# A convolution tile whose pads change places: one POOL copy less, one written by ScalarE from PSUM instead

## The chip, the cores and the metric

The kernel runs on one core of one Trainium2 chip. The metric is the time of one execution on the device in microseconds (us). TensorE (PE in the profile) multiplies matrices and writes PSUM; VectorE (DVE), ScalarE (ACT) and GpSimd (POOL) work elementwise; SyncE (SP) issues the DMAs. Each engine takes its own instructions strictly in the order of the program and waits on semaphores for the others.

## What is computed

The reference is one inference step of a small hybrid decoder: a Mamba-2 layer, an attention layer, and an MLP behind each. There are 1024 prompt tokens, 8 samples of 8 new tokens, and 16 meta tokens that stand ahead of the prompt. Only the first layer's causal convolution is touched by the change:

```python
def mamba_mixer(h, conv_state, ssm_state, norm_w, w_in, conv_w, conv_b, ...):
    zxbcdt = rmsnorm(h, norm_w) @ w_in
    ...
    xpad = jnp.concatenate([conv_state.astype(xbc.dtype), xbc], axis=1)
    new_conv = xpad[:, L:]
    conv = conv_b
    for k in range(CONV_K):
        conv = conv + xpad[:, k:k + L] * conv_w[k]
    xbc = jax.nn.silu(conv)
    ...
```

`CONV_K` is 4, so each output needs the three inputs before it. For a sample these are three rows of `state_conv`. For the meta tokens they are zeros. For the prompt they are the last three meta rows, since the prompt goes on from the meta tokens' state. `new_conv`, the last three inputs, is an output for the prompt and for each sample.

## The kernel before

Features lie on the 128 partitions and tokens along the columns: columns 0 to 1023 are the prompt, then 64 sample columns, then 16 of meta, 1104 in all (`T`). PE works on three chunks of columns, `CH`: 384, 384 and 336, the last with 256 prompt columns and the 80 others. The fp32 products are made as three products of split halves (`mm3`, L205 to L207), 24 matmuls for a unit's chunk.

The work before some 680 us is `mixer` (L1956). It goes through 8 groups, and each has four *units* of 128 features: B, C, x0 and x1. A unit is made so:

- `conv_unit` (L553) takes its weights, a tile `xp` of two buffers for the unpadded product with its pads, and a tile `fm` (called `acc` there) for the result.
- `conv_mm` (L560) makes a chunk's product in one of three PSUM banks `g`. Chunks go in the order 2, 0, 1 (`CORD`), so the samples and meta tokens come first.
- `conv_out` (L583) empties the bank with ScalarE. L588 copies prompt columns to `xp`. For the chunk with the others L590 copies the 80 columns into ten blocks of eight, each behind three columns of pad. L592 writes the last tap and the bias into `acc`, and with that the bank is free.
- `conv_rest` (L595) has POOL fill the pads and the output `cvo` of new states: L600 puts the samples' states into blocks 0 to 7, L601 puts zeros ahead of the first meta block (8), L602 copies the end of block 8 ahead of the second meta block (9), L603 copies the end of block 9 ahead of the prompt, and L604 and L605 copy the new states out. Then DVE does three short taps over the 80 columns (L608), three long taps over the 1024 (L611), and the gate (L615) around ScalarE's tanh (L614).

The state-space part of a group, `ssd` (L627), runs beside the units of the *next* group. It is a recurrence over nine stretches of tokens (first the 80 others, then eight of 128), made of small PE matmuls: transposes into `tp` (L647 to L649), `cb` (L659), `y` (L675 and L679), the carried state through `st` (L701, L708; DVE adds it at L703 and L713, POOL scales it at L710). For the samples, PE makes their state update in `st` (L767, L768), POOL scales the old state `h` in four pieces (L759), and DVE adds the two (L769). There is one PSUM bank `st`, so L767 and L708 wait until the last user of `st` is read. POOL also makes `xd` (L657) and `bm` (L754) and ends the output `yt` (L694). In the last group the gate's units take the place of the convolution's (`gate_group`, L773): their products meet DVE at L788, L789 and L797, and a sum over features goes through ScalarE (L248), DVE (L249) and PE (L260, L263).

What sets the order: the kernel is written as a stream of operations, and a scheduler places them on each engine by a simulated time line, each as early as its inputs and buffers allow there. The order of an engine is then fixed, and semaphores do the rest. So a change of one operation can move others on every engine.

## Time and profile before

| | before |
|---|---|
| time, median of 3 runs | 2843.23 us (2842.11 to 2844.07) |
| the profiled execution | 2845.32 us, span of its instructions 2843.6 us |
| mean granted TensorE clock | 0.995 |
| busy: PE, DVE, ACT, POOL | 98%, 73%, 49%, 17% of the span |
| instructions on POOL | 659 |

In the profile, busy is the union of an engine's instructions. PE's ends are modelled, so that neighbouring matmuls overlap: the distance from start to start is what one costs. "Idle before" is the time that the engine stood still ahead of an instruction, and the name behind the arrow is what ended that wait. An instruction between two long ones can show a wait that costs nothing, because only waits that reach PE move the end here. Instructions with fp32 operands count twice on PE. All times within the execution are from the span's start.

### The profile page before, as it was taken

How to read it: one execution, taken by the hardware profiler on the slowest of the kernel's cores; microseconds unless marked ns; L12 is line 12 of the kernel's file. 1: busy time of each engine (PE TensorE's matmuls, PEld its weight loads, DVE VectorE, ACT ScalarE, POOL GpSimd, SP SyncE). 2: the span in 40 equal slices, each digit the busy share in tenths (PEclk: the TensorE clock that was granted, in tenths of full speed). 3: DMA queues.
4: the chain of work that ended last, by engine and by line, in shares of the span. 5: the costliest groups of instructions: out<-in, count | busy, mean ns of one | idle time of the engine just before them, and what ended most of it. 6: DMA issues, size and time to landing. Idle time of an engine off the chain costs nothing.

```text
span 2843.6 us, 51263 instructions
## 1 busy us (share of the span) xinstructions
PE 2788.5 (98%) x19861; PEld 2690.4 (95%) x19861; DVE 2069.6 (73%) x3603; ACT 1392.0 (49%) x2721; POOL 476.2 (17%) x659
## 2 busy tenths in 40 slices
PE   8999999999999999999999999999999999999998
PEld 7999989988999999999999999988989999999998
DVE  6788878887768786666578875676678666577785
ACT  6555555555664355445343334555545445433333
POOL 3355555552000100000000022110110000000011
PEclk9999999999999999999999999999999999999999
DMA  4354444456755223533654533447553444543332
GB/s 140 93 149 125 129 121 111 126 147 206 272 204 183 91 93 128 182 129 129 238 212 173 178 115 91 165 167 255 169 181 115 157 159 149 201 153 132 128 124 78
DMA packets 219467, 433.41 MB, mean 152 GB/s; under 512 B 30728, under 2 KB 128392, under 8 KB 216648
## 3 DMA queue, kind: packets, MB, share of 16 engines
q1 hardware_dynamic: 219224, 430.14, 45.4%
q8 instruction: 156, 2.56, 0.4%
q14 instruction: 87, 0.71, 0.1%
HBM read 302.71 MB, written 128.32 MB: 152 GB/s over the span
## 4 chain that ended last, share of the span: by engine, by line
PE 82%; DVE 7%; DMA 5%; issue 2%; ACT 2%; POOL 1%; SPq 0%; POOLq 0%; DVEq 0%; ACTq 0%
PE g L206 11%; PE g L205 11%; PE g L207 11%; PE ma L205 4%; PE mc L205 4%; PE mc L207 4%; PE mc L206 4%; PE ma L207 4%; PE ma L206 4%; PE mb L207 3%; PE mb L206 3%; PE md L206 3%; PE mb L205 3%; PE md L207 3%; PE md L205 3%
## 5 line engine op out<-in xcount | busy, mean ns | idle before, releaser
L205 PE MATMUL g<-S,w 128*128 128x384 f32 (+2 forms) x1584 | 534.0, 337 | 3.6 <-DMA w<-ws_up 2.0
L206 PE MATMUL g<-S,w 128*128 128x384 f32 (+2 forms) x1584 | 532.3, 336 | 0.0
L207 PE MATMUL g<-S,w 128*128 128x384 f32 (+2 forms) x1584 | 531.1, 336 | 0.0
L205 PEld LDWEIGHTS g<-S,w 128*128 128x128 f32 x1584 | 300.0, 189 | 7.1 <-issue 3.9
L1091 ACT CAST w<-s 128x384 fp32r<-128x384 f32 (+1 forms) x272 | 150.4, 557 | 318.1 <-DVE s L1222 56.9
L206 PEld LDWEIGHTS g<-S,w 128*128 128x128 f32 x1584 | 300.5, 190 | 3.3 <-issue 2.6
L207 PEld LDWEIGHTS g<-S,w 128*128 128x128 f32 x1584 | 300.9, 190 | 2.5 <-issue 1.8
L1342 POOL TENSOR_TENSOR hh<-hh,us 128x552 f32<-128x552 f32 (+1 forms) x24 | 42.5, 1789 | 1528.8 <-DVE us L1318 872.8
L205 PE MATMUL ma<-S,w 128*128 128x276 f32 (+1 forms) x808 | 233.6, 289 | 4.0 <-DVE us L1318 2.7
L206 PE MATMUL ma<-S,w 128*128 128x276 f32 (+1 forms) x808 | 233.2, 289 | 0.3 <-DVE S L1280 0.3
L207 PE MATMUL ma<-S,w 128*128 128x276 f32 (+1 forms) x808 | 233.4, 289 | 0.0
L1092 DVE TENSOR_TENSOR w<-s,w 128x384 fp32r<-128x384 f32 (+1 forms) x272 | 166.5, 616 | 81.2 <-ACT w L1091 81.2
L1091 ACT CAST w<-raw 128x384 fp32r<-128x384 f32 (+1 forms) x204 | 112.2, 556 | 180.0 <-PE mc L207 54.1
L171 ACT CAST w<-raw 128x1024 fp32r<-128x1024 f32 x96 | 100.6, 1048 | 140.4 <-PE g L206 48.7
L172 DVE TENSOR_TENSOR w<-raw,w 128x1024 fp32r<-128x1024 f32 x96 | 123.0, 1281 | 48.4 <-ACT w L171 30.1
L206 PE MATMUL g<-R,w 128*128 128x384 f32 (+2 forms) x480 | 158.1, 329 | 0.0
L205 PE MATMUL g<-R,w 128*128 128x384 f32 (+2 forms) x480 | 158.0, 329 | 0.0
L207 PE MATMUL g<-R,w 128*128 128x384 f32 (+2 forms) x480 | 157.7, 329 | 0.0
L205 PEld LDWEIGHTS ma<-S,w 128*128 128x128 f32 x808 | 152.1, 188 | 4.9 <-ACT w L1091 3.1
L206 PEld LDWEIGHTS ma<-S,w 128*128 128x128 f32 x808 | 152.2, 188 | 0.5 <-DVE S L1280 0.5
L207 PEld LDWEIGHTS ma<-S,w 128*128 128x128 f32 x808 | 152.1, 188 | 0.0
L206 PE MATMUL mc<-S,w 128*128 128x276 f32 (+1 forms) x512 | 148.0, 289 | 0.7 <-DVE S L1280 0.7
(488 smaller groups left out, 8506.6 us busy)
## 6 DMA issues: line engine op xcount, KB each, us to landing
raw<-in_w_up_dram SPq DMA_DIRECT2D x64, 512.0 KB
raw<-in_w_in_dram SPq DMA_DIRECT2D x48, 512.0 KB
raw<-in_w_downs_dram SPq DMA_DIRECT2D x64, 384.0 KB
w<-ws_o SPq DMA_DIRECT2D x46, 512.0 KB
w<-ws_q SPq DMA_DIRECT2D x40, 512.0 KB
ab<-acs_d SPq DMA_DIRECT2D x64, 256.0 KB
S<-t_d SPq DMA_DIRECT2D x18, 828.0 KB
S<-t_e SPq DMA_DIRECT2D x18, 816.0 KB
```

Of the source, the lines that this page charges most:

```text
L171: nc.scalar.copy(out=wh, in_=raw)
L172: nc.vector.tensor_tensor(out=wl, in0=raw, in1=wh.bitcast(F32), op=ALU.subtract)
L205: mm(out=out, lhsT=wh, rhs=xh, start=(first and k == 0), stop=False)
L206: mm(out=out, lhsT=wh, rhs=xl, start=False, stop=False)
L207: mm(out=out, lhsT=wl, rhs=xh, start=False, stop=(k == n - 1))
L1091: self.last_hi = nc.scalar.copy(out=t[:, 0], in_=src).ins
L1092: self.last_lo = nc.vector.tensor_tensor(out=t[:, 1], in0=src, in1=t[:, 0].bitcast(F32), op=ALU.subtract).ins
L1342: e.tensor_tensor(out=to, in0=to, in1=uv, op=ALU.add)
```

## The change

The two parts of `xp` change places. Before, it held the pad and the prompt first (`XB` = 1027 columns) and then the ten padded blocks of samples and meta (110 columns). After it, the ten blocks come first (`XB` = 110) and the prompt's 1024 columns follow directly. Block 9 ends with the last eight meta rows, so the three columns ahead of the prompt are by themselves its pad, and the copy L603 goes. The pad of block 9, the last three rows of block 8, is written by ScalarE straight from the PSUM bank in `conv_out`, a copy of 128x3 behind the one of 128x80, and POOL's copy L602 goes. The taps read the same number of columns from their new places, and the tile has 1134 columns where it had 1137.

```diff
-XB = 3 + SEQ
-XW = XB + 110
+XB = 110
+XW = XB + SEQ
...
-        nc.scalar.copy(out=xp[:, 3 + o:3 + o + m], in_=pt[:, :m])
+        nc.scalar.copy(out=xp[:, XB + o:XB + o + m], in_=pt[:, :m])
         if m < n:
-            nc.scalar.copy(out=xp[:, XB:XW].rearrange("p (b e) -> p b e", e=11)[:, :, 3:11],
-                           in_=pt[:, m:n].rearrange("p (b q) -> p b q", q=8))
+            tail = xp[:, :XB].rearrange("p (b e) -> p b e", e=11)
+            nc.scalar.copy(out=tail[:, :, 3:11], in_=pt[:, m:n].rearrange("p (b q) -> p b q", q=8))
+            nc.scalar.copy(out=tail[:, 9, 0:3], in_=pt[:, m + 69:m + 72])
...
-        tail = xp[:, XB:XW].rearrange("p (b e) -> p b e", e=11)
+        tail = xp[:, :XB].rearrange("p (b e) -> p b e", e=11)
         nc.gpsimd.tensor_copy(out=tail[:, 0:8, 0:3], in_=cv[:, j, 5:29].rearrange("p (b k) -> p b k", k=3))
         nc.gpsimd.memset(tail[:, 8, 0:3], 0.0)
-        nc.gpsimd.tensor_copy(out=tail[:, 9, 0:3], in_=tail[:, 8, 8:11])
-        nc.gpsimd.tensor_copy(out=xp[:, 0:3], in_=tail[:, 9, 8:11])
-        nc.gpsimd.tensor_copy(out=self.cvo[:, j, 0:3], in_=xp[:, SEQ:SEQ + 3])
+        nc.gpsimd.tensor_copy(out=self.cvo[:, j, 0:3], in_=xp[:, XW - 3:XW])
...
-            nc.vector.scalar_tensor_tensor(out=acc[:, :SEQ], in0=xp[:, k:k + SEQ], scalar=cv[:, j, k:k + 1],
+            nc.vector.scalar_tensor_tensor(out=acc[:, :SEQ], in0=xp[:, XB - 3 + k:XB - 3 + k + SEQ], scalar=cv[:, j, k:k + 1],
```

Counted over the 32 units, POOL loses 64 copies, ScalarE gains 32, and every other instruction stays. The scheduler places the work anew on all engines from the first units (about 34 us of the profile before) to the end of the mixer (about 675 us); behind that the orders are equal. The lines below `conv_rest` move up by one, so L769 of before is L768 after. Three places matter below.

The first is the fifth group's sample states, at about 390 to 405 us of the profile before. On POOL stood, ahead of and behind the scaling of the old state (L759; its tile `h_4444` is one group's state):

```order
L754 TENSOR_TENSOR bm<-bhl,bsel 128x1024
L694 TENSOR_TENSOR yt<-yt,yo 128x256
L759 TENSOR_TENSOR h_4444<-h_4444,eendb 128x8x64 x4
L710 TENSOR_TENSOR hT<-hT,eend 128x256
L604 COPY cvo<-xp 128x3
L602 COPY xp<-xp 128x3
L603 COPY xp<-xp 128x3
L605 COPY cvo<-xp 128x24
```

There stands now, on the same engine at the same place:

```order
L693 TENSOR_TENSOR yt<-yt,yo 128x256
L656 TENSOR_TENSOR xd<-xdt,de 80x256
L753 TENSOR_TENSOR bm<-bhl,bsel 128x1024
L758 TENSOR_TENSOR h_4424<-h_4424,eendb 128x8x64 x4
L709 TENSOR_TENSOR hT<-hT,eend 128x256
L603 COPY cvo<-xp 128x3
L604 COPY cvo<-xp 128x24
```

The sum into `yt` has moved ahead of `xd` and `bm`, and of the copies only the two into `cvo`, which nothing on DVE waits for, are left. DVE at this place, before:

```order
L661 TENSOR_TENSOR cbm<-cb,tri 128x128
L611 SCALAR_TENSOR_TENSOR fm<-xp,cv,fm 128x1024
L738 TENSOR_TENSOR yo<-pp,ef 128x64 x2
L608 SCALAR_TENSOR_TENSOR fm<-xp,cv,fm 128x80 x2
L769 TENSOR_TENSOR h_4444<-h_4444,st 128x512
L608 SCALAR_TENSOR_TENSOR fm<-xp,cv,fm 128x80
L615 SCALAR_TENSOR_TENSOR fm<-th,fm 128x1104
```

And now:

```order
L660 TENSOR_TENSOR cbm<-cb,tri 128x128
L607 SCALAR_TENSOR_TENSOR fm<-xp,cv,fm 128x80
L737 TENSOR_TENSOR yo<-pp,ef 128x64 x2
L607 SCALAR_TENSOR_TENSOR fm<-xp,cv,fm 128x80 x2
L614 SCALAR_TENSOR_TENSOR fm<-th,fm 128x1104
L768 TENSOR_TENSOR h_4424<-h_4424,st 128x512
```

The short taps and the gate of the unit now stand ahead of the state update. On PE the product that waits for this update (L767) has 13 more of the large matmuls ahead of it than before.

The second place is PE at about 661 to 665 us, near the end of the last group. Before:

```order
L768 MATMUL st<-xdl,bm 128x256
L679 MATMUL y<-fm,hT 128x128 x2
L708 MATMUL st<-xd,Bt 128x256
L260 MATMUL g<-msh,ones_r 128x384
L205 MATMUL g<-S,w 128x336
L206 MATMUL g<-S,w 128x336
```

Now:

```order
L767 MATMUL st<-xdl,bm 128x256
L678 MATMUL y<-fm,hT 128x128 x2
L260 MATMUL g<-msh,ones_r 128x384
L205 MATMUL g<-S,w 128x336
L206 MATMUL g<-S,w 128x336
```

The product into `st` (L708, now L707) stands 22 large matmuls further on, and the sum over features (L260) comes first.

The third place is POOL at the start of the last group's recurrence, about 606 to 616 us. Before:

```order
L694 TENSOR_TENSOR yt<-yt,yo 128x256
L657 TENSOR_TENSOR xd<-xdt,de 80x256
L759 TENSOR_TENSOR h_7088<-h_7088,eendb 128x8x64 x4
L754 TENSOR_TENSOR bm<-bhl,bsel 128x1024
L710 TENSOR_TENSOR hT<-hT,eend 128x256
```

Now:

```order
L693 TENSOR_TENSOR yt<-yt,yo 128x256
L758 TENSOR_TENSOR h_7056<-h_7056,eendb 128x8x64 x4
L656 TENSOR_TENSOR xd<-xdt,de 80x256
L753 TENSOR_TENSOR bm<-bhl,bsel 128x1024
L656 TENSOR_TENSOR xd<-xdt,de 128x256
```

The scaling has moved ahead of the 80-row product `xd`, from which PE makes the first carried state (L701).

## Prediction

> **What bounds the kernel now.** First the page: span, engines, and the chain that ended last.

> ```profile
> span 2843.6 us, 51263 instructions
> PE 2788.5 (98%) x19861; PEld 2690.4 (95%) x19861; DVE 2069.6 (73%) x3603; ACT 1392.0 (49%) x2721; POOL 476.2 (17%) x659
> PE 82%; DVE 7%; DMA 5%; issue 2%; ACT 2%; POOL 1%; SPq 0%; POOLq 0%; DVEq 0%; ACTq 0%
> ```

> TensorE is the bound, and POOL, which loses work, carries 1% of the chain. Next the windows of the first 680 us, because the changed functions run only in the mixer: the copies of the first row below last from 34 to 591 us. In the other rows the columns are the window, its length, and busy us with instruction counts for PE, weight loads, DVE, ACT and POOL, then the granted clock and DMA.

> ```profile
> L588 ACT COPY xp<-g x96: 348/471/488, 34.2 to 591.2; 128x384 f32<-128x384 f32 x64, 128x256 f32<-128x256 f32 x32
> ...
> 100.00:200.00 100.00, 100.00 (x690) 92.10 (x690) 80.21 (x140) 57.61 (x139) 56.35 (x76) 1.00 0.50 133
> 400.00:500.00 100.00, 97.36 (x655) 90.19 (x654) 77.81 (x136) 52.84 (x124) 48.98 (x80) 0.98 0.45 130
> 600.00:680.00 80.00, 72.77 (x482) 65.38 (x481) 65.42 (x123) 41.90 (x95) 31.73 (x36) 0.98 0.49 143
> ```

> In most of the mixer PE has no idle time at all, so taking work from POOL, DVE or ACT is worth nothing there. What can be won is the 2.6 us in the window from 400 and part of the 7.2 us in the last 80. The waits of PE up to 680 us name them (engine, tile and line, releaser, us in total, times, longest):

> ```profile
> PE st L708 <- DVE h L769: 3.2, 1, 3.2
> PE st L767 <- DVE h L769: 3.0, 2, 2.6
> PE g L260 <- ACT msh L248: 2.5, 2, 1.7
> ```

> The second row holds the stall at 402 us. The timelines of PE, DVE and POOL at that place show its cause.

> ```profile
> 401.99 0.34 PE L206 MATMUL g<-S,w 128*128 128x384 f32 x1
> 404.98 0.39 PE L767 MATMUL st<-xdh,bm 128*128 128x256 f32 x1 [2.64 <-DVE h L769]
> ...
> 398.54 0.34 DVE L738 TENSOR_TENSOR yo<-pp,ef 128x64 f32<-128x64 f32 x2
> 403.39 0.93 DVE L608 SCALAR_TENSOR_TENSOR fm<-xp,cv,fm 128x80 f32<-128x80 f32 x2 [4.51 <-POOL xp L602]
> 404.25 0.68 DVE L769 TENSOR_TENSOR h<-h,st 128x512 f32<-128x512 f32 x1
> ...
> 391.81 5.73 POOL L694 TENSOR_TENSOR yt<-yt,yo 128x256 f32<-128x256 f32 x1 [1.40 <-DVE yt L690]
> 397.50 5.03 POOL L759 TENSOR_TENSOR h<-h,eendb 128x512 f32<-128x512 f32 x4
> 402.49 0.61 POOL L710 TENSOR_TENSOR hT<-hT,eend 128x256 f32<-128x256 f32 x1
> 403.05 0.18 POOL L604 COPY cvo<-xp 128x3 f32<-128x3 f32 x1
> 403.18 0.18 POOL L602 COPY xp<-xp 128x3 f32<-128x3 f32 x1
> ```

> A copy of 0.18 us stood in POOL's queue behind 11 us of other work. DVE waited 4.51 us for it at the tail's taps (L608). The state update L769, next in DVE's queue, came late, and PE, whose L767 needs the bank that L769 frees, stood still for 2.64 us.

> The stall has a second price. The clock column, window by window:

> ```profile
> 402.00:405.00 3.00, 0.36 (x3) 0.03 (x2) 1.57 (x4) 0.54 (x1) 2.23 (x9) 1.00 0.23 53
> 406.40:409.80 3.40, 3.40 (x16) 2.96 (x16) 0.88 (x2) 0.27 (x1) 0.61 (x1) 0.51 0.06 10
> 409.80:413.20 3.40, 3.40 (x28) 3.23 (x25) 2.41 (x6) 2.63 (x6) 1.20 (x2) 1.00 0.07 11
> 662.40:665.80 3.40, 1.23 (x7) 1.18 (x8) 3.40 (x9) 1.56 (x4) 0.45 (x1) 0.99 0.63 243
> 665.80:669.20 3.40, 3.40 (x14) 3.40 (x13) 3.40 (x7) 0.52 (x1) 1.93 (x3) 0.50 0.83 302
> ```

> From 406.4 us on the granted clock was 0.51 for 3.4 us, and the same followed the long stall near 662 us. About half the matmuls fit: an estimate of 3.4 x (1 - 0.51) = 1.7 us lost at most. I take 1.5.

> **The change, part by part.** *Removed from POOL*: 32 L602 and 32 L603. The groups by line (count | busy us, mean ns | idle before):

> ```profile
> L602 POOL COPY xp<-xp 128x3 f32<-128x3 f32 x32 | 13.0, 406 | 0.3 <-DVE xdt L652 0.3
> L603 POOL COPY xp<-xp 128x3 f32<-128x3 f32 x32 | 7.8, 242 | 0.0
> DVE fm L608 <- POOL xp L602: 10.3, 11, 4.5
> ```

> That is 20.8 us of POOL, worth nothing by itself, and 10.3 us of DVE's waiting in 11 places (last row). Ten of them never reached PE. The eleventh is the stall at 402 us. What is late there next? L769 also needs POOL's L759, which ended at 402.53 and does not go away. So L769 can end at about 402.53 + 0.68 = 403.2 rather than 404.93. In the new order 13 more matmuls stand ahead of this L767, at 0.18 us from start to start (two neighbours, below), or 2.3 us. PE gets there at about 404.4, after L769. The wait should vanish.

> ```profile
> 615.03 0.34 PE L206 MATMUL g<-S,w 128*128 128x384 f32 x1
> 615.21 0.34 PE L207 MATMUL g<-S,w 128*128 128x384 f32 x1
> 617.21 0.44 PE L260 MATMUL g<-msh,ones_r 128*128 128x384 f32 x1 [1.65 <-ACT msh L248]
> ...
> 608.73 4.05 POOL L759 TENSOR_TENSOR h<-h,eendb 128x512 f32<-128x512 f32 x4
> ```

>  The row's other 0.4 us (one L767 near 263 us) is covered in the same way by 5 matmuls. **-3.0 us**, between -3.0 and 0: nothing if L759 is held up longer, and no further gain exists in this row. With the stall its slow clock goes: **-1.5 us**, between -1.7 and 0, since other stalls may sit in another phase.

> [...] Here the clock fell after a stall of 2.64 us, so in this trace a mostly idle window sufficed. [...]

> *Added to ScalarE*: 32 copies of 128x3 from PSUM, between the 128x80 copy and the activation that closes the bank. The nearest rows:

> ```profile
> 34.50 0.23 ACT L590 COPY xp<-g 128x80 f32<-128x80 f32 x1
> 34.62 0.65 ACT L592 ACTIVATE fm<-g,cv 128x336 f32<-128x336 f32 x1
> ```

> The 128x80 copy lasted 0.23 us but held the next instruction back by only 0.12 us. For 32 copies that is 3.8 us (7.4 us by the duration). I take 0.12 as what ScalarE's queue sees. ScalarE is 53 to 58% busy here and PE has three banks to turn over, so the bank's release 0.12 us later is hidden: **0**. Without that cover it would be +3.8 us; it cannot fall below zero, since nothing leaves this queue. The tail's taps now wait for this copy instead of POOL's. It lies directly behind the copies they need anyway, so nothing long is queued ahead.

> *Moved*: the pad and the sequence change places in one tile. The sequence taps read as many columns as before, so they stay at their price: **0**. What POOL still writes ahead of the taps (the sample states and zeros) depends only on the buffer being free, as before.

> *Reordered*: the scheduler places everything anew up to 675 us, not beyond. Most of PE's dependent small matmuls come 3 to 15 large ones later, which is slack. In the order of the whole mixer I count 12 more switches between large and small matmuls; eight of these are y blocks that are followed directly by a large one. **+0.5 us**, an estimate, between 0 and 2. In the last 80 us the order around PE's longest wait changes:

> ```profile
> 663.20 0.50 ACT L248 CAST msh<-gt 128x384 fp32r<-128x384 f32 x1
> ...
> 663.85 0.67 DVE L769 TENSOR_TENSOR h<-h,st 128x512 f32<-128x512 f32 x1
> ...
> 664.57 0.70 PE L708 MATMUL st<-xd,Bt 128*128 128x256 f32 x2 [3.15 <-DVE h L769]
> ```

> L708 now stands behind L260 and 22 matmuls, so L769 has time. L260, which stands first now, needs L248, whose end at 663.70 leaves a wait of about 2.3 us where there were 3.15: **-1.0 us**. In return the last group starts its recurrence later: POOL's scaling of the carried state (4.05 us at 608.73, above) now stands ahead of the 80-row product that starts it. I count **+0.5 us** for a wait that opens near 629 us, between 0 and +4, the length of that POOL block. The tail's bounds are then -4.7 (both stalls and the second slow clock) and +4.

> Sum: -3.0 - 1.5 + 0.5 - 1.0 + 0.5 = **-4.5 us**. The profiled execution took 2845.3 us (span 2843.6 and 1.7 around it), 2.1 above the runs' median, so it would come to 2840.8, and the median of 2843.2 to **2838.7 us**.

> **The rivals.** *Given back (2843 us)*: the 402 us stall goes but the new order opens others of like size, since a wait of 2 us anywhere in 640 us suffices. For it: PE waits for several kinds of small result in every group, and each place was set anew. Against it: most of them moved later, and before, with the same work, the waits table has one wait of over 2 us that lies ahead of the last 80 us. -4.5 + 4.3, about 2843.

> *The tail gains too (2834 us)*: L708's stall goes with its slow clock, and L260's wait of 1.65 us at 617.21 shrinks because POOL's scaling starts earlier there. -4.5 - 2.3 - 1.5 - 0.9 = -9.2. For it: 22 matmuls are plenty. Against it: DVE is busy in all 3.40 us of the window from 662.4, and something must wait for it.

> *POOL starved (2849 us, slower)*: DVE no longer pauses at L608, and those pauses are when POOL's two-input work got through. The row of the added squares shows how the two engines hold each other up:

> ```profile
> L797 DVE TENSOR_TENSOR gt<-gt x6: 500/668/4796, 608.4 to 682.1; 128x384 f32<-128x384 f32 x4, 128x336 f32<-128x336 f32 x2
> ```

> One of six took 4.80 us beside POOL's scaling, as L694 took 5.73 us beside DVE. The scaling stands between the bank's update and PE in each of 8 groups. If it is starved once more in three groups by 3 to 4 us beyond the 1 to 2 us of slack, PE loses about 2.5 us in each and has a slow clock in two: 7.5 + 3.0 - 4.5 = +6.0, 2849.2. It decides from about 2 us of delay on. [...] Against the rival: 20.8 us of POOL's own work go.

> *The clock is not the stall's doing (2840 us)*: it fell 1.4 us after PE had started again (404.98 to 406.4) and may fall once more somewhere here whatever PE does. Then only the wait is saved: -4.5 + 1.5 = -3.0, 2840.2. [...] Against it: both slow windows of the table stand right behind PE's two longest waits.

> **How the numbers follow.** Forecast 0.45, given back 0.22, tail gains 0.17, starved 0.11, clock independent 0.05. What a measurement of this kernel can tell from no change is about 0.2%, 5.7 us: below 2837.5 is faster, above 2848.9 slower. Faster: the tail's case, and a third of the forecast's (its terms reach -7), 0.32. Slower: most of the starved case and a little of the given-back, 0.09. Same: 0.59. The range runs from the tail's case, 2834.0, to 2846.0, which takes in the given-back case with 3 us of spread and leaves out the starved one.

> **What would show it.** Right: no wait of 2 us at L767 in the fifth group, DVE not waiting for POOL at the tail's taps, no granted clock near 0.5 between 400 and 420 us, POOL some 20 us less busy, and the end of the mixer 3 to 5 us earlier. Wrong: a new wait of PE for the state update, long two-input POOL instructions, or the gain lost again behind the mixer, whose order is unchanged.

## The result and the profile after

The changed kernel took 2834.23 us in the median of five runs (2828.37 to 2835.08), the kernel before 2843.23 in five beside them (2840.14 to 2845.05). The ratio is 0.9962, with a 95% interval of 0.9951 to 0.9973: some 0.4% faster, 9.0 us by the medians and 10.8 by the ratio. The forecast was -4.5 us. First the page of the profiled execution, which was the shortest of its five runs (2828.37 us, 5.9 below their median), so the 17.3 us between the two spans say too much:

```profile
span 2826.3 us, 51212 instructions
...
PE 2780.6 (98%) x19861; PEld 2686.2 (95%) x19861; DVE 2068.0 (73%) x3603; ACT 1391.9 (49%) x2753; POOL 469.9 (17%) x595
...
PE 87%; DVE 5%; DMA 4%; ACT 2%; issue 1%; POOL 0%; SPq 0%; POOLq 0%; DVEq 0%; ACTq 0%
```

PE has gone from 82% to 87% of the chain, and POOL from 1% to none. POOL is 6.3 us less busy, not 20. The waits of PE up to 680 us (in the changed kernel the lines behind the convolution have numbers one lower: L768 is the L769 of before, L766 and L767 the old L767 and L768, L707 the old L708; ScalarE's new copy is L592):

```profile
PE g L260 <- ACT msh L248: 2.3, 3, 1.3
...
PE g L578 <- DVE S L365: 0.4, 1, 0.4
PE y L674 <- DVE dec L668: 0.3, 1, 0.3
```

None is for the state update any more. Before, there were 7.8 us of waits for `st` in three rows, the two that the prediction shows (3.2 and 3.0) and this one:

```profile
PE st L767 <- DVE hT L713: 1.6, 2, 1.0
```

The windows of the changed kernel, two of them those of the forecast, the others around PE's longest wait in the tail:

```profile
400.00:500.00 100.00, 100.00 (x693) 92.64 (x692) 81.08 (x139) 54.61 (x134) 50.09 (x66) 1.00 0.49 135
600.00:680.00 80.00, 77.37 (x514) 70.97 (x513) 59.91 (x117) 46.69 (x97) 32.79 (x33) 1.00 0.58 181
652.10:655.50 3.40, 2.11 (x14) 2.07 (x14) 3.40 (x8) 0.92 (x2) 0.00 (x0) 1.00 0.67 257
655.50:658.90 3.40, 3.40 (x27) 2.98 (x25) 2.78 (x7) 1.69 (x3) 2.63 (x2) 1.00 0.87 332
```

PE lost 2.64 us in the window from 400 and now loses none. It lost 7.2 in the last 80 and now loses 2.6, and the granted clock is 1.00 in both. The place at 402 us, PE, DVE and POOL:

```profile
403.17 0.28 PE L766 MATMUL st<-xdh,bm 128*128 128x256 f32 x1
...
398.57 0.87 DVE L607 SCALAR_TENSOR_TENSOR fm<-xp,cv,fm 128x80 f32<-128x80 f32 x1
399.37 0.34 DVE L737 TENSOR_TENSOR yo<-pp,ef 128x64 f32<-128x64 f32 x2
399.63 1.39 DVE L607 SCALAR_TENSOR_TENSOR fm<-xp,cv,fm 128x80 f32<-128x80 f32 x2
400.94 1.29 DVE L614 SCALAR_TENSOR_TENSOR fm<-th,fm 128x1104 f32<-128x1104 f32 x1
402.16 0.67 DVE L768 TENSOR_TENSOR h<-h,st 128x512 f32<-128x512 f32 x1
...
392.33 8.02 POOL L758 TENSOR_TENSOR h<-h,eendb 128x512 f32<-128x512 f32 x4 [1.73 <-PE po L725]
400.31 0.61 POOL L709 TENSOR_TENSOR hT<-hT,eend 128x256 f32<-128x256 f32 x1
400.87 0.20 POOL L603 COPY cvo<-xp 128x3 f32<-128x3 f32 x1
```

The tail's taps (L607) start without a wait while POOL is still in its scaling (L758). The state update ends at 402.83, and PE's L766 starts at 403.17 without a wait. The margin is 0.34 us.

The scaling took 8.02 us where it had taken 5.03, but at this place nobody waits for it. That goes with its new place beside DVE's long taps (L610, 1.27 us each at 391.61, 394.40 and 397.17), where before the sum L694 stood and took 5.73 us (0.73 where it stands now). That DVE no longer pauses isn't the reason: in the run *before_in_new_order* below DVE stands still for 2.57 us behind the long taps, and the scaling takes 8.01 us all the same; in *both_in_old_order* it takes 5.03.

To see where the time went in spite of single executions that differ by some us, I take the start of the n-th matmul record in each trace. Every trace has 19861 of them, and the 4400th lies behind the last place where the two orders differ. Before, the 1000th, 2600th, 3800th and 4400th start at 175.7, 411.6, 587.2 and 685.4 us. After, they start at 174.1, 406.0, 580.7 and 672.7. So the stretch with the stall at 402 us (1000th to 2600th) became 4.0 us shorter, the middle (2600th to 3800th) 0.9, and the tail (3800th to 4400th) 6.2: together 11.1, which accounts for the change. What follows behind the mixer differs by up to some 6 us between the executions below, whatever the kernel.

### The profile page after: what moved, and what is told of

Read it like the earlier page. It is cut to its first block, busy times and chain, and to the rows that moved or that the text cites. A ratio compares the mean times of both kernels' runs of the same rounds, so it can differ in the third digit from the quotient of the medians.

```text
span 2826.3 us, 51212 instructions
## 1 busy us (share of the span) xinstructions
PE 2780.6 (98%) x19861; PEld 2686.2 (95%) x19861; DVE 2068.0 (73%) x3603; ACT 1391.9 (49%) x2753; POOL 469.9 (17%) x595
## 4 chain that ended last, share of the span: by engine, by line
PE 87%; DVE 5%; DMA 4%; ACT 2%; issue 1%; POOL 0%; SPq 0%; POOLq 0%; DVEq 0%; ACTq 0%
PE g L207 12%; PE g L206 12%; PE g L205 12%; PE mc L205 4%; PE mc L207 4%; PE mc L206 4%; PE ma L205 4%; PE ma L207 4%; PE ma L206 4%; PE mb L207 3%; PE md L206 3%; PE mb L206 3%; PE mb L205 3%; PE md L207 3%; PE md L205 3%; PE y L674 1%
## 5 line engine op out<-in xcount | busy, mean ns | idle before, releaser
L206 PE MATMUL g<-S,w 128*128 128x384 f32 (+2 forms) x1584 | 532.7, 336 | 0.0
L207 PE MATMUL g<-S,w 128*128 128x384 f32 (+2 forms) x1584 | 531.6, 336 | 0.0
L207 PEld LDWEIGHTS g<-S,w 128*128 128x128 f32 x1584 | 299.9, 189 | 3.8 <-issue 2.6
L206 PEld LDWEIGHTS g<-S,w 128*128 128x128 f32 x1584 | 299.5, 189 | 3.1 <-issue 2.5
L207 PE MATMUL ma<-S,w 128*128 128x276 f32 (+1 forms) x808 | 233.8, 289 | 0.0
L206 PE MATMUL ma<-S,w 128*128 128x276 f32 (+1 forms) x808 | 233.4, 289 | 0.0
L172 DVE TENSOR_TENSOR w<-raw,w 128x1024 fp32r<-128x1024 f32 x96 | 129.3, 1347 | 45.5 <-ACT w L171 34.5
L206 PE MATMUL g<-R,w 128*128 128x384 f32 (+2 forms) x480 | 158.3, 330 | 0.0
L207 PE MATMUL g<-R,w 128*128 128x384 f32 (+2 forms) x480 | 157.9, 329 | 0.0
L206 PEld LDWEIGHTS ma<-S,w 128*128 128x128 f32 x808 | 152.5, 189 | 0.0
L207 PEld LDWEIGHTS ma<-S,w 128*128 128x128 f32 x808 | 152.3, 188 | 0.0
```

Of the source, the lines that this page charges most:

```text
L172: nc.vector.tensor_tensor(out=wl, in0=raw, in1=wh.bitcast(F32), op=ALU.subtract)
L206: mm(out=out, lhsT=wh, rhs=xl, start=False, stop=False)
L207: mm(out=out, lhsT=wl, rhs=xh, start=False, stop=(k == n - 1))
```

## The experiments

Two tools serve below. The first is the scheduler: ScalarE's copy alone (run *act_copy_only*) makes it place everything as in the changed kernel, and without that copy (*layout_only*) it places everything as before. The second holds an order fixed: a table of instruction numbers, engine by engine, and an ordering edge without a semaphore from each to the next.

```diff
+def _pin(tc, nc):
+    ...
+            if last:
+                tc.add_manual_dep(traced[name], last, mybir.DependencyInfo(mybir.DependencyClass.NoSync, mybir.DependencyReason.DATA),
+                                  reason="order")
+            last = name
```

So the edits can be tried in the old order and the new order without the edits. All runs were compared with the kernel before on the same chip in five rounds. The three columns behind the ratio are the stretches of the profiled execution against before (235.9, 175.6 and 98.2 us), worked out as above.

| run | ratio, 95% interval | 402 us stretch | middle | tail |
|---|---|---|---|---|
| changed kernel | 0.9962, 0.9951 to 0.9973 | -4.0 | -0.9 | -6.2 |
| layout_only | 1.0000, 0.9991 to 1.0008 | -0.1 | 0.0 | -0.3 |
| act_copy_only | 0.9958, 0.9944 to 0.9972 | -4.0 | -0.9 | -6.2 |
| both_in_old_order | 0.9986, 0.9977 to 0.9994 | -3.9 | 0.0 | +1.4 |
| before_in_new_order | 0.9981, 0.9972 to 0.9990 | -1.9 | +2.3 | -5.9 |
| one_matmul_moved | 1.0003, 0.9993 to 1.0013 | -1.5 | 0.0 | -0.6 |
| two_waits_moved | 0.9997, 0.9988 to 1.0005 | -2.7 | 0.0 | +0.7 |
| after_one_back | 0.9974, 0.9964 to 0.9983 | -4.0 | -0.9 | -2.9 |
| after_nudged | 0.9966, 0.9953 to 0.9979 | -4.0 | -0.9 | -6.1 |
| new_order_behind_645 | 0.9996, 0.9987 to 1.0005 | 0.0 | 0.0 | -1.5 |
| xd_behind_scaling | 1.0003, 0.9994 to 1.0012 | -1.5 | 0.0 | -0.7 |
| xd_ahead_of_scaling | 0.9959, 0.9946 to 0.9971 | -4.0 | -0.9 | -3.7 |
| act_copy_four_times | 0.9958, 0.9946 to 0.9970 | -4.0 | -0.9 | -6.1 |
| new_order_behind_602 | 0.9981, 0.9973 to 0.9990 | 0.0 | 0.0 | -6.0 |
| old_order_behind_602 | 0.9981, 0.9972 to 0.9990 | -4.0 | -0.9 | +1.9 |

The medians behind these ratios lie between 2831.1 and 2845.0 us; those of before, in the experiments, between 2842.1 and 2844.3. In the kernels of the experiments the lines have the numbers of the kernel before.

**Each edit alone.** *layout_only* leaves out the ScalarE copy and keeps POOL's L602:

```diff
-            nc.scalar.copy(out=tail[:, 9, 0:3], in_=pt[:, m + 69:m + 72])
...
+        nc.gpsimd.tensor_copy(out=tail[:, 9, 0:3], in_=tail[:, 8, 8:11])
```

> Samples in front, so 32 of POOL's L603 are gone; L602 stays on POOL and ScalarE gets no copy. Every other instruction of all engines stands where it stood before. Theory copy (the gain is DVE's freedom from POOL's L602) and theory order (the gain is the new places of the work): both no change, 2843 within 2 us, with the stall of 2.6 us at 402 us and its slow clock still there. Theory relief (any copy less on POOL helps DVE and POOL through): some 3 us faster, a third of the 20.8 us of copies being gone.

Nothing changed, and the stall is there as before:

```profile
PE st L767 <- DVE h L769: 3.0, 2, 2.5
```

So a third of POOL's small copies is worth nothing by itself: the theory of relief falls. *act_copy_only* keeps the old places in the tile:

```diff
+            nc.scalar.copy(out=xp[:, XB:XW].rearrange("p (b e) -> p b e", e=11)[:, 9, 0:3], in_=pt[:, m + 69:m + 72])
...
-        nc.gpsimd.tensor_copy(out=tail[:, 9, 0:3], in_=tail[:, 8, 8:11])
```

> ScalarE writes the pad of block 9 from PSUM, the pad of the sequence is still copied by POOL (L603). The order of all engines is that of the changed kernel, with L603 in it. Theory copy and theory order: the whole gain, 2834 within 2 us. Theory relief: some 3 us of the gain is missing, 2837.

It has the whole gain, stretch by stretch. Of the change, only L602's way to ScalarE counts.

**The edits and the order apart.** *both_in_old_order* is the changed kernel held in the old order, *before_in_new_order* the kernel before held in the new one.

> The changed kernel's instructions, held in the order of the kernel before on every engine (only ScalarE's 32 new copies find their own place). Theory copy: nearly the whole gain, 2835. Theory order: at 402 us DVE's update ends at about 403.2, and PE, which comes 13 matmuls earlier than in the new order, still waits about 0.9 us; the slow clock there goes; in the last 80 us all stays, with PE's wait of 3.2 us and its slow clock: -1.7 - 1.5, about 2840.

> The instructions of the kernel before, both POOL copies among them and no copy on ScalarE, held in the order of the changed kernel on every engine. Theory copy: DVE waits for POOL's L602 as before, the time stays at 2843 within 2 us. Theory order: at 402 us DVE's update is as late as before, at about 404.9, but PE comes 13 matmuls or 2.3 us later and waits some 0.5 us; the last 80 us are as in the changed kernel. Most of the gain without any of the edits: 2835 to 2836.

Neither theory had it alone. Each half gives about half: ratios of 0.9986 and 0.9981, -4.0 and -5.4 us. The waits of PE in the old order with the edits:

```profile
PE st L708 <- DVE h L769: 3.2, 1, 3.2
PE g L260 <- ACT msh L248: 2.5, 2, 1.6
...
PE st L767 <- DVE h L769: 1.0, 1, 1.0
```

The stall at 402 us has shrunk from 2.6 to 1.0 (0.9 was expected) without a slow clock behind it. The tail's longest waits are untouched, and its +1.4 comes with a second slow stretch of the clock (from 614.5 us, beside the one from 662.3). And in the new order without the edits:

```profile
PE tp L647 <- DVE yo L738: 4.2, 3, 1.4
PE g L260 <- ACT msh L248: 2.4, 3, 1.3
```

The tail is as in the changed kernel (-5.9), but a new wait stands in the groups. Its cause, on DVE and POOL at the first of its three places:

```profile
398.65 0.27 DVE L661 TENSOR_TENSOR cbm<-cb,tri 128x128 f32<-128x128 f32 x1
401.49 0.32 DVE L608 SCALAR_TENSOR_TENSOR fm<-xp,cv,fm 128x80 f32<-128x80 f32 x1 [2.57 <-POOL xp L602]
401.74 0.34 DVE L738 TENSOR_TENSOR yo<-pp,ef 128x64 f32<-128x64 f32 x2
...
401.27 0.18 POOL L602 COPY xp<-xp 128x3 f32<-128x3 f32 x1
```

DVE waits for POOL's L602 again, and now it is L738 behind the taps that comes late, for whose bank PE's transposes L647 wait. So the edit removes a wait of DVE that reaches PE in either order, only at other places, and the tail belongs to the order alone.

**Single moves.** *one_matmul_moved* is the kernel before with L708 at 661 us put behind L260 and 22 large matmuls; *two_waits_moved* moves also the four matmuls of the stall at 402 us 13 later. Only the table differs; on PE, with the rows of the second move first:

```diff
-L767 MATMUL st<-xdh,bm 128x256
-L768 MATMUL st<-xdl,bm 128x256
-L767 MATMUL st<-xdh,bm 128x256
-L768 MATMUL st<-xdl,bm 128x256
 L205 MATMUL g<-S,w 128x384
 ...
+L767 MATMUL st<-xdh,bm 128x256
+L768 MATMUL st<-xdl,bm 128x256
+L767 MATMUL st<-xdh,bm 128x256
+L768 MATMUL st<-xdl,bm 128x256
 L675 MATMUL y<-dec,xdt 128x128
...
-L708 MATMUL st<-xd,Bt 128x256
 L260 MATMUL g<-msh,ones_r 128x384
 ...
+L708 MATMUL st<-xd,Bt 128x256
```

> The kernel before, every engine held in its old order, but for one matmul: the L708 that waits 3.15 us at 661 us stands behind L260 and 22 large matmuls, as in the new order. No copy is moved. Prediction's step: ScalarE and DVE keep their order, so L260's operand (L248) still ends at 663.7 and L260 waits about 2.2 us in L708's place: -0.9 us, 2842, with the slow clock still behind it. Rival (tail gains, L708's wait goes and nothing takes its place): -3.2 - 1.5, 2838.5.

> As the one before it, and the four matmuls of L767 and L768 that wait 2.64 us at 402 us also stand 13 large matmuls later, as in the new order. POOL's copies stay. Theory order: PE comes 2.3 us later to a bank that is free as late as before, waits some 0.3 us and keeps its clock there: -2.3 - 1.6 = -3.9 on top of the run before, about 2838. Theory copy: DVE is still held up by POOL's L602, the wait only moves: no more than -0.5 on top.

The first did what the prediction's step says for it. Its waits from 600 to 700 us:

```profile
PE g L260 <- ACT msh L248: 5.6, 3, 2.3
PE st L767 <- DVE hT L713: 1.2, 2, 1.0
```

L260 waits 2.3 us in L708's place, the slow clock stays, and the tail is 0.6 us shorter. The second took PE's wait for L769 down to 0.4 us, but another took its place, so that half of the stall came back:

```profile
PE y L675 <- DVE xdt L652: 1.0, 1, 1.0
PE st L767 <- DVE h L769: 0.4, 1, 0.4
```

Both times are those of before within the interval. In the second run's trace the 402 us stretch is 2.7 us shorter, 1.25 of it in the waits and some 1.5 in a clock that stayed up, but the tail lost 0.7 with a second slow stretch (from 615.5 us). So a late DVE is cured at most in part by moving one of PE's rows. These runs also show the slow clock apart from its stall. In *one_matmul_moved* nothing is changed at 402 us and the stall is 2.65 us, yet the clock stayed up. First that run, then before, by the windows of the clock:

```profile
398.60:402.00 3.40, 2.27 (x15) 1.91 (x13) 0.07 (x1) 1.05 (x2) 3.40 (x8) 1.00 0.71 207
402.00:405.40 3.40, 1.88 (x12) 1.88 (x13) 3.36 (x7) 0.14 (x1) 0.86 (x6) 1.00 0.15 33
405.40:408.80 3.40, 3.40 (x29) 2.98 (x28) 1.44 (x5) 1.74 (x6) 0.52 (x1) 1.00 0.01 3
```

```profile
399.60:403.00 3.40, 2.73 (x17) 2.37 (x15) 0.00 (x0) 1.23 (x3) 3.40 (x4) 1.00 0.73 222
403.00:406.40 3.40, 1.42 (x9) 1.43 (x10) 2.97 (x6) 0.00 (x0) 1.23 (x8) 0.99 0.13 30
```

In before, one window held 1.98 us of the stall (PE busy 1.42 of 3.40), and the next was slow. In the other run two windows shared the stall (busy 2.27 and 1.88), and none was slow. The clock is worth 1.5 us, the -1.5 of that run's first stretch. Of the six executions with this stall unchanged, four had the slow clock behind it.

*after_one_back* is the changed kernel with its L707 put ahead of L260 again, *after_nudged* a try for more: the changed kernel with the L260 and L263 behind the mixer, at 745 and 779 us, up to 20 matmuls later. The first one's move, and the last of the second's:

```diff
+L708 MATMUL st<-xd,Bt 128x256
 L260 MATMUL g<-msh,ones_r 128x384
 ...
-L708 MATMUL st<-xd,Bt 128x256
...
-L260 MATMUL ms<-msh,ones_r 128x336
 ...
+L260 MATMUL ms<-msh,ones_r 128x336
```

> The changed kernel in its own order, but for one matmul: the L707 (before: L708) stands ahead of L260 again. DVE's update ends there at about 655.0, PE comes at 652.1: a wait of 2.9 us in place of L260's 1.3, and the slow clock behind it: +1.6 + 1.7 = +3.3 us, 2837.5. If a wait of under 3 us is made up for by what follows: 2834.

```profile
PE st L708 <- DVE h L769: 3.0, 1, 3.0
PE g L260 <- ACT msh L248: 1.1, 2, 0.8
```

The wait of 3.0 us is back, the slow clock behind it too (at 655.3), and the tail is 3.3 us longer (-2.9 for -6.2), as worked out.

> The changed kernel in its own order, but behind the mixer the L260 that waits 2.1 us at 745.6 us (with the two of its kind behind it) stands some 7 to 17 large matmuls later and the L260 and L263 at 779 us, where PE waits 2.7 us with a slow clock behind it, 20 later. If a wait of PE is worth its row and its slow clock wherever it is: -2.1 - 2.7 - 1.6 = -6.4, about 2828. If what hangs on these sums of squares (ScalarE's L816 and the DMAs behind it) is then late for later weights: no change, 2834.

This gave nothing. L263, right behind, now waits for DVE's half of the same sum. From 680 to 960 us PE's waits sum to 7.9 us, in the changed kernel to 7.4. The waits from 700 to 800 us:

```profile
PE ms L263 <- DVE msl L249: 2.8, 1, 2.8
```

**POOL's block in the tail.** In before, DVE's add of squares L797 took 4.80 us beside POOL's scaling. In the changed kernel (there L796) it takes 0.65. *xd_behind_scaling* puts, in the kernel before, POOL's 80-row L657 behind the scaling and its three users later; *xd_ahead_of_scaling* puts it ahead in the changed kernel. On POOL the first is this, and the second the reverse:

```diff
-L657 TENSOR_TENSOR xd<-xdt,de 80x256
 L759 TENSOR_TENSOR h<-h,eendb 128x512
 ...
+L657 TENSOR_TENSOR xd<-xdt,de 80x256
 L754 TENSOR_TENSOR bm<-bhl,bsel 128x1024
```

> The kernel before in its old order, but POOL's 80-row product L657 at 608.2 us stands behind the four L759, as in the new order; the three instructions that use it (two casts of ScalarE, L752 of DVE) stand behind L248 and L249. If the meeting of POOL's block with DVE's add of squares L797 makes that add last 4.80 us: L797 takes 0.6 us, L260's wait of 1.65 us at 617 us goes, -1.7 us, 2841.5. If the long L797 comes from the add's own start, whatever POOL does first: L797 stays at 4.80 us, no change, 2843.

> The changed kernel in its own order, but POOL's 80-row product stands ahead of the four scalings again, in the last group. If POOL's order makes DVE's add of squares long: the add L797 (here at 601 us) takes 4 to 5 us, PE waits 1.7 us at L260: +1.7, 2836. Else 2834.

In the first, L797 fell to at most 0.97 us and L260's wait of 1.65 us went, but PE waited for the moved product instead, some 4 us earlier: a wait for a wait, no gain.

```profile
610.61 0.69 PE L701 MATMUL st<-xd,Bt 16*128 16x256 f32 x2 [1.64 <-POOL xd L657]
```

In the second, it is not L797 that was long but the next DVE instruction, 4.39 us to the end of POOL's block:

```profile
602.27 0.65 DVE L797 TENSOR_TENSOR gt<-gt 128x384 f32<-128x384 f32 x1
603.15 4.39 DVE L746 TENSOR_TENSOR bhl<-Bt,bhl 64x128 fp32r<-64x128 f32 x1 [0.23 <-ACT bhl L745]
...
602.46 0.93 POOL L657 TENSOR_TENSOR xd<-xdt,de 80x256 f32<-80x256 f32 x1
603.36 4.04 POOL L759 TENSOR_TENSOR h<-h,eendb 128x512 f32<-128x512 f32 x4
```

L260 then waits 2.2 us, and the tail is 2.5 us longer than in the changed kernel. The median doesn't show that loss (0.9959 beside 0.9962, each by 0.0012): it is smaller than what the intervals tell apart.

**ScalarE's price.** The copy is made four times, in the changed kernel's own order.

```diff
-            nc.scalar.copy(out=tail[:, 9, 0:3], in_=pt[:, m + 69:m + 72])
+            for _ in range(4): nc.scalar.copy(out=tail[:, 9, 0:3], in_=pt[:, m + 69:m + 72])
```

> The changed kernel in its own order, with ScalarE's 128x3 copy made four times, 96 copies more. Prediction: the bank's release some 0.36 us later is hidden behind PE's other banks, 2834 (the change then paid nothing for its 32). If the bank's release is on PE's path: 96 x 0.12 = +11.5 us, 2845.5, and the 32 copies of the change cost 3.8.

Nothing moved: the three stretches are those of the changed kernel within 0.1 us. The timeline shows what the four last, 0.66 us from the first to the start of the activation behind them, 0.17 each where 0.12 was taken:

```profile
395.91 0.76 ACT L591 COPY xp<-g 128x3 f32<-128x3 f32 x4
396.57 0.64 ACT L592 ACTIVATE fm<-g,cv 128x336 f32<-128x336 f32 x1
```

**Where the order's gain lies.** *new_order_behind_645* and *new_order_behind_602* are the kernel before, in the old order up to that time and in the new one behind it; *old_order_behind_602* is the changed kernel, in the new order up to there and in the old one behind it.

> The kernel before, with both its POOL copies, in its old order up to 645 us and in the new order behind that: 88 matmuls and 24 instructions of the other engines stand elsewhere, all between 645 and 680 us. Prediction's step for this place: L708's wait of 3.15 us gives way to a wait of 2.3 us at L260 and the slow clock stays: -1.0 us, 2842. Rival (the tail gains): L260 waits 1.3 us as in the changed kernel's trace and the clock stays up: -1.9 - 1.6 and the 0.6 us wait of L767 = about -4, 2839.

> The kernel before, with both its POOL copies, in its old order up to 602 us and in the new order behind that: 275 matmuls and some 150 instructions of the other engines stand elsewhere. Theory tail (the gain is the arrangement of the last 80 us itself): L260's wait of 1.65 us goes, L708's 3.15 us give way to 1.3 us at L260, no slow clock near 660 us: some -6 between 602 and 680 us, 2837. Theory prediction (something must wait there): no more than -1, 2842.

> The changed kernel in its own order up to 602 us and in the old order behind that. Theory tail: the waits of 1.65 and 3.15 us and the slow clock near 660 us come back, of the change's gain the part up to 602 us stays (the stall at 402 us, its slow clock and about 1 us more): -4 to -5 against the kernel before, 2838.5. Theory prediction: the gain up to 602 us is nearly all of it, 2835.

Behind 645 us alone it gives -1.5: L260 waits 2.0 us there, and the next window is slow.

```profile
661.00:664.40 3.40, 1.56 (x10) 1.56 (x11) 3.40 (x8) 0.92 (x2) 0.00 (x0) 0.99 0.56 217
664.40:667.80 3.40, 3.40 (x14) 3.40 (x13) 2.77 (x9) 0.52 (x1) 1.70 (x1) 0.50 0.89 345
```

Behind 602 us it gives the whole -6.0, with not one edit, and its waits from 600 to 700 us are those of the changed kernel:

```profile
PE g L260 <- ACT msh L248: 2.4, 3, 1.3
PE y L675 <- DVE dec L669: 0.3, 1, 0.3
```

With the old order put back there, the tail even costs 1.9 us more than before, since a second slow clock stands in it (at 614.8 us, beside the one at 662.6) and L260's first wait is 2.5 us instead of 1.65. The two halves are 0.9981 each, -5.4 us each, and their sum is the change's 10.8.

## Why the prediction was wrong

The direction and the mechanism at 402 us were right; the size was wrong by a factor of two.

- *The stall at 402 us, -3.0, and its slow clock, -1.5.* Right. The stretch became 4.0 us shorter in every run that has both the copy on ScalarE and the new order there. But the margin was nearly used up. DVE's update was to end 1.2 us ahead of PE (403.2 and 404.4), worked out from POOL's scaling as the last thing that it waits for. It ended 0.34 us ahead (402.83 and 403.17; this execution is 1.6 us early from its first part on, so only the distances compare). It stood behind DVE's own taps and gate, which the new order puts ahead of it (the gate L614 alone takes 1.29 us) and which the prediction left out. That the clock's part hangs on the phase was in the bounds (0 to -1.7); it came in four of six executions. In before, the window ahead of the slow one had PE busy for 1.42 of 3.40 us.
- *The tail, -1.0 and +0.5, measured -6.2.* **This is the step that failed**: "L260, which stands first now, needs L248, whose end at 663.70 leaves a wait of about 2.3 us where there were 3.15", with the slow clock left standing. The 2.3 were worked out from PE's new order and the old times of DVE and ScalarE. For that mixture it was right: with one matmul moved and all else in place, L260 waited 2.3 us. But DVE's, ScalarE's and POOL's orders behind 602 us had changed too. Together they bring L260's operand earlier against PE (with the new order behind 645 us alone it still waits 2.0 us, so part of this lies between 602 and 645 us; which engine's order does it wasn't taken apart): it waits 1.3 us, its window is not slow, its earlier wait of 1.65 us at 617 us is down to 0.3, and PE's two waits for L713 (1.6 us) are gone. By the rows that is 3.2 + 2.5 + 1.6 of waits before less 2.3 + 0.3 after, 4.7 us, and some 1.6 for the slow clock, against 6.2 measured. The new wait near 629 us (+0.5) didn't come. The bound of -4.7 for the tail, "both stalls and the second slow clock", is also too tight by the prediction's own rows: 3.15 + 1.65 + 1.5 = 6.3.
- *The switches, +0.5.* Nothing bears this term out. The matmul records have 68 changes from a large to a small product in the middle where there were 53, and the middle, for which I had no term, became 0.9 us shorter. By the distances from start to start there in before, a large product ahead of a small one took 197 ns and a small one ahead of a large one 63, together 260; large ahead of large and small ahead of small took 175 and 107, together 282. So a change costs nothing by this estimate (the shapes differ). No wait of PE stands in the middle in either kernel, and where its 0.9 us come from stays open.
- *ScalarE's copies at nothing.* Right, with room: 96 more also cost nothing.
- *POOL some 20 us less busy.* Wrong. The rows of L602 and L603 are gone, but the copy behind them, L605 (L604 in the changed kernel), became dearer. The groups of POOL's copies up to 680 us, before and then after:

```profile
L604 POOL COPY cvo<-xp 128x3 f32<-128x3 f32 x32 | 19.8, 619 | 51.0 <-ACT xp L588 51.0
...
L605 POOL COPY cvo<-xp 128x24 f32<-128x24 f32 x32 | 8.3, 260 | 0.0
```

```profile
L604 POOL COPY cvo<-xp 128x24 f32<-128x24 f32 x32 | 20.0, 624 | 0.3 <-DVE xdt L651 0.3
L603 POOL COPY cvo<-xp 128x3 f32<-128x3 f32 x32 | 19.5, 611 | 50.0 <-ACT xp L588 49.9
```

  With the 20.8 us of L602 and L603 the four summed to 48.9 us, the two now to 39.5, 9.4 less. Up to 680 us all of POOL is 10.4 us less busy (335.9 and 325.5). Behind that, where the order is the same, it was 4.1 us busier in this execution (140.3 and 144.4), which leaves the 6.3.
- *The rivals.* *The tail gains too* was what happened, and for its reason; its counterargument, that something must wait while DVE is busy, holds only for the 1.3 us. That its -9.2 lies beside -9.0 by the medians is partly luck: its tail is -5.2, measured -6.2, and the middle isn't in it. *POOL starved* came at one place, with the scaling of 8.02 us, but by the scaling's new place and not for want of DVE's pauses, and no one was waiting. *The clock is not the stall's doing* falls: from 60 to 680 us before has two slow stretches, and in the 3.41 us ahead of each PE stood still for 2.0 us or more (busy for 1.37 us from 402.94 and for 1.20 from 662.35). The changed kernel has no such window there (the least busy has 2.12, from 652.07) and no slow stretch. *Given back* didn't come; where it would have come is shown by the copies left on POOL in the new order: +2.3 in the middle.

## What to carry to other kernels

Where a scheduler sets the order, a small edit is two changes, and the second can be as large as the first; holding either order fixed by a table tells them apart in two runs. When you work out a wait in a new order, take both sides of it from that order: moving the waiting row alone found the next late operand in both runs that tried it. And where a kernel bound by PE shows a slow clock behind its stalls, as this one did, count it for each stall as a chance, not as a sum: the stall of 2.6 us at 402 us had one behind it in four of six executions, and the wait of 2.0 us in *new_order_behind_645* had one too.
